# Quarter loads of the down projection on GpSimd's queue, its seven-product groups later, one transposed block turned later

## Chip, cores and metric

The kernel runs on one core of one Trainium2 chip. The metric is the device time of one execution in microseconds (us), lower is better; the time of a version is the median of its runs.

## What is computed

One layer of a decoder trunk, 256 tokens, 2048 channels, all float32:

```
h = rmsnorm(x) * w;  proj = h @ w_in                        # 2048 x 14368
two token mixers (gated delta rule, causal pooling) from proj, merged by gates -> mixed
x = x + mixed @ w_out                                       # 2048 x 2048
h = rmsnorm(x) * w
gate, up = split(h @ w_up)                                  # 2048 x 2*5632
gate = causal depthwise conv(gate, 3 taps) + bias
x = x + (gelu(gate) * up) @ w_down                          # 5632 x 2048
y = rmsnorm(x) * w_final
```

The change touches the last output block of `mixed @ w_out`, the start of `h @ w_up`, and the product with `w_down`.

## The kernel before

**Products.** TensorE multiplies in float32r. To keep float32 accuracy, each operand is split into a high part and a low part (value less high part). For one weight block of 256 rows x 512 columns (two slices of 128 rows), each of the two token tiles of 128 takes six matmuls of 512 columns: high x high, low x high and high x low for each slice (`products`, L1295, for the down projection; `high_first`, used at L1313, for up). So a plain block is 12 matmuls.

**Weights.** All blocks of the whole kernel stand in one list, `srcs`, in the order in which TensorE uses them. `weights()` (L167) hands out the next block and makes sure that blocks two further on are begun. `begin` (L240) does for each block: load it (SP issues the DMA, 512 KB, L179, into one of four `raw` buffers), copy the high part on ACT (`whi`, L253), subtract on VectorE (`wlo`, L261). There are three buffers each of `whi` and `wlo`, so a cast waits until TensorE is through with the block three before it. A block that is used at the very end is kept in a buffer of its own (`khi`, `klo`), cast among the others.

**Seven products.** In three of the eleven 512-row chunks of the down projection (`SEVEN`, chunks 8, 9 and 10), a 2 x 2 product of halves is done with seven products instead of eight: 11, 21, 22, T1, T3, T2, T4 (`PRODUCTS`), six matmuls each. This needs sums on both sides:
- of the weights: two loads of 1 MB each (`quad`, L209, in the big buffers x1 and x2) bring four quarters of 256 x 512; VectorE forms the four sums in place (L246), and each of the seven is split like a block;
- of the tokens: `half_sums` (L1237) forms four sums on VectorE (L1226 to L1229) and splits them (L1230, L1231).

A quarter's buffer can be loaded again when the last product from it has been split: x1 after T3, x2 after T4. The buffers x1 and x2 held features 4 to 7 and 8 to 11 of the up projection before.

**Order of the down projection.** It goes in two halves of 1024 columns. `stream` (L128) lays out each half: `gaps` gives how many plain blocks come before each of the three groups, each product of a group but the first is followed by one plain block, and what is left of the 32 plain blocks of the first half comes last. Before: gaps (4, 2, 2) in the first half, (3, 1, 1) in the second, where four kept blocks are put in too. The last up tile's gate and up parts (transposes at L341, then `gate_part` and `up_part`) are done behind the first and second plain block. In the code, `quarter` issues the two loads when it is asked for "11", on SP; `half_sums` of the next group is called at the "11" of the group before it.

**Banks.** Results are summed in PSUM: `psm` (two buffers of two banks) and `psg` (four banks). In the first half 11, T1, T3 and T2 have the psg banks, which are freed by a chain of sums on VectorE after T4 of the third group; the second half's plain blocks sum in psg.

**The output projection.** It makes four blocks of 512 columns. For each: a product, the residual added on VectorE into `xt` (L1194), the sum stored to HBM (`xtd`, ACT's queue), squares on ACT, eight transposes on TensorE (L1204) into psg, and the high and low part of the features `fhl` (L1209, L1210). Then come the up blocks, whose first ones read features 0 to 3. The buffer of `xt` then serves for quarters of the up projection, and after the last of these the residual is read back from `xtd` with four loads on ACT (L1412); the weights of the last norm follow (`nfin`, L1414).

**Who orders.** Buffers, waits and the order on each engine come from a scheduler, which follows a timeline of its own and can pull an instruction ahead of its place in the code; for TensorE's up stage the order is written out by hand.

Of the kernel before, what the change touches and what calls it, by code (L numbers as in the profile page):

```python
# [8 lines left out]
F32 = mybir.dt.float32  # L9
# [3 lines left out]
ALU = mybir.AluOpType  # L13

P = 128
# [20 lines left out]
def kernel(  # L36
# [91 lines left out]
    def stream(half, direct, gaps, keeps=()):  # L128
        todo = [(kp, c) for d in direct for kp in (2 * d, 2 * d + 1) for c in (2 * half, 2 * half + 1)]
        used = [0]  # L130

        def plain(n):
            for _ in range(n):
                kp, c = todo.pop(0)
                steps[half].append(("plain", kp, c))
                srcs.append(down[c][kp])
                used[0] += 1
                if used[0] in keeps:
                    i = keeps.index(used[0])
# [12 lines left out]
        plain(len(todo))  # L152

    ends = [(2 * d + j, c) for d in LAST for c in (2, 3) for j in range(2)]
    stream(0, DIRECT, (4, 2, 2))
    stream(1, DIRECT[:-2], (3, 1, 1), (9, 13, 17, 21))
    srcs += [down[c][kp] for kp, c in ends[:4]]
    made = []
# [21 lines left out]

    quarters = {}
    up_quarters = {}
    last_quad_split = [None]
    UP_BUFFER = {"11": 0, "T1": 1, "T2": 1, "T3": 0, "21": 2, "22": 3, "T4": 1}

    def quad_load(c, n):
# [8 lines left out]
    def up_sum(what):  # L195
        b11, b12, b21, b22 = (up_quarters[i] for i in range(4))
        for out_, plus_, minus_ in {"T1": [(b12, b12, b11)], "T2": [(b12, b22, b12)],
                                    "T3": [(b11, b12, b11), (b12, b21, b12)]}[what]:
            nc.vector.tensor_tensor(out_, plus_, minus_, op=ALU.subtract)  # L199

    def quarter(half, chunk, what):

        if half == "up":
            return up_quarters[UP_BUFFER[what]]
        if what == "11":
            for j in range(2):
                r = big.tile([P, 2, 1024], F32, tag=f"x{1 + j}", name=nm("quad"))
                rows = slice((2 * chunk + j) * 256, (2 * chunk + j + 1) * 256)
                last_load[0] = nc.sync.dma_start(r, w_down[0, rows, half * 1024 : (half + 1) * 1024]  # L209
                                                 .rearrange("(k p) f -> p k f", p=P)).ins  # L210
                for i in range(2):
                    quarters[j, i] = r[:, :, 512 * i : 512 * (i + 1)]
        b11, b12, b21, b22 = (quarters[j, i] for j in range(2) for i in range(2))
        sums = {"T1": (b11, b12, b11), "T3": (b12, b22, b12), "T2": (b22, b22, b11), "T4": (b21, b21, b22)}
        return sums[what] if what in sums else quarters[int(what[0]) - 1, int(what[1]) - 1]
# [24 lines left out]
    def begin(n):  # L240
        while len(made) < min(len(srcs), n):
            load(len(made) + 1)
            raw = loads[len(made)]
            if isinstance(raw, tuple):
                raw, plus, minus = raw
                nc.vector.tensor_tensor(raw, plus, minus, op=ALU.subtract)  # L246
            src = srcs[len(made)]
            following = {"T1": "T2", "T2": "T3"}.get(src[2]) if isinstance(src, tuple) and src[0] == "up" else None
            shape = list(raw.shape)
            keep = kept.get(len(made))  # L250
            hi = wpool.tile(shape, F32R, tag="whi", name=nm("whi")) if keep is None else \
                mtile(keep, shape, F32R, nm("khi"))
            nc.scalar.copy(hi, raw)  # L253
            if shape[1] == 8:
                lo = None
                nc.vector.tensor_tensor(hi[:, :, 32:64], raw[:, :, 0:32], hi[:, :, 0:32].bitcast(F32),
                                        op=ALU.subtract)
            else:
                lo = wpool.tile(shape, F32R, tag="wlo", name=nm("wlo")) if keep is None else \
                    mtile(4 + keep, shape, F32R, nm("klo"))  # L260
                last_split[0] = nc.vector.tensor_tensor(lo, raw, hi.bitcast(F32), op=ALU.subtract).ins  # L261
                splits.append(last_split[0])
            made.append((hi, lo))
            if following is not None:
                up_sum(following)
            if isinstance(src, tuple) and src[2] == "T4":
                last_quad_split[0] = last_split[0]


    side_work = [iter(())]  # L270
# [8 lines left out]
    def pm():  # L279
        return psm.tile([P, 2, 512], F32, tag="m", name=nm("psm"))  # L280
# [114 lines left out]
    def both(parts, k):  # L395
        return parts[k // 4][:, k % 4]
# [791 lines left out]
    for c in range(4):  # L1188
        if c < 2:
            ps = gemm_a(at(mhi), at(mlo), KD, range(6, 8), early[c])  # L1190
        else:
            ps = gemm_a(at(mhi), at(mlo), KD)
        xs = xt[:, :, c * 512 : (c + 1) * 512]
        nc.vector.tensor_tensor(xs, xs, ps, op=ALU.add)  # L1194
        nc.scalar.dma_start(xt_d[:, :, c * 512 : (c + 1) * 512], xs)
        for t in range(2):
            jk = cpool.tile([P, 512], F32, tag="sqj", name=nm("sqj"))
            nc.scalar.activation(jk, xs[:, t, :], AF.Square, accum_out=ssq4[:, t, c : c + 1])
        for k2 in range(2):
            pt = pg([P, 2, S])  # L1200
            for kk in range(2):
                k = 4 * c + 2 * k2 + kk
                for t in range(2):
                    nc.tensor.transpose(pt[:, kk, t * P : (t + 1) * P], xt[:, t, k * P : (k + 1) * P], ident)  # L1204
            for kk in range(2):
                k = 4 * c + 2 * k2 + kk
                nw = vec[:, V_FFN + k : V_FFN + k + 1]
                high, low = (both(fhl, k)[:, n, :] for n in range(2))
                nc.scalar.activation(high, pt[:, kk, :], AF.Copy, scale=nw)  # L1209
                nc.vector.scalar_tensor_tensor(low, pt[:, kk, :], nw, high.bitcast(F32),  # L1210
                                               op0=ALU.mult, op1=ALU.subtract)
# [169 lines left out]
    for i, step in enumerate(up_steps):  # L1381
        if step[0] == "part":
            up_product(*step[1:])
            if step[2] == "T4":
                def elementwise(c=step[1] - 1, gates=gates, ups=ups):
                    yield from gate_part(c, gates)
                    up_part(c, ups)
                    yield

                work[:] = [elementwise()]  # L1390
        elif step[0] == "gate":
            gates = turned_pair(pending[step[1], 0])
        elif step[0] == "up":
            ups = turned_pair(pending[step[1], 1])
        elif step[0] == "plain":
            up_plain(*step[1:])
            if step[1] == 0 and step[2:] == (0, TAIL):
                up_ups.append(up_sums())
            if step[1] == NUP - 1 and step[2:] == (0, KD // 2 - 1):
                half_sums(SEVEN[0])  # L1400
            if work:
                next(work[0], None)
        for n in range(4):
            if i + 8 - n < len(up_steps) and up_steps[i + 8 - n][0] == "loads":
                quad_load(up_steps[i + 8 - n][1], n)
        if i + 3 < len(up_steps) and up_steps[i + 3][0] == "loads":
            up_sum("T1")
    pe_order.close()

    xt = fp.tile([P, 2, D], F32, tag="xt", name="xt")  # L1410
    for c in range(4):
        nc.scalar.dma_start(xt[:, :, c * 512 : (c + 1) * 512], xt_d[:, :, c * 512 : (c + 1) * 512])  # L1412
# [32 lines left out]
    for hf in range(2):  # L1445
# [9 lines left out]
            bank_of |= zip(("11", "T1", "T2", "T3"), other)  # L1455
        began = set()
        for n, step in enumerate(steps[hf]):
            if hf == 0 and n == 1:
                for _ in gate_part(NUP - 1, turned(pending[NUP - 1, 0])):
                    pass  # L1460
# [13 lines left out]
            chunk, what = step[1:]  # L1474
            if what not in bank_of:
                bank_of[what] = pg()
            if hf == 0 and what == "11" and chunk != SEVEN[-1]:
                half_sums(SEVEN[SEVEN.index(chunk) + 1])
            which = OPERAND[what]
            if isinstance(which, tuple):  # L1480
# [117 lines left out]
```

## Time and profile before

| | us |
|---|---|
| median of 3 runs (lowest, highest) | 1553.15 (1551.57, 1554.37) |
| the profiled execution | 1552.89 |
| its span | 1551.2 |
| TensorE (PE) busy | 1538.3 |
| VectorE (DVE) busy | 1195.5 |
| ScalarE (ACT) busy | 827.5 |
| GpSimd (POOL) busy | 44.7 |
| output projection ends, up stage begins | at about 818 |
| down projection begins | at about 1306 |
| last products end | at about 1537 |

The granted TensorE clock is full but for the last stretch. HBM is read at 199 GB/s on average over the span. The profile comes from one execution. Times in it are counted from the start of its span. Rows of the timeline have start, duration, engine, line, operation, out<-in, shapes, count, and in brackets the engine's idle time ahead of it and what ended it. PEld is TensorE's weight load, SPq and ACTq are instructions of SP's and ACT's queue, that issue DMAs. Matmul ends are modelled, so pauses of TensorE are best read from the starts.

### The profile page before, as it was taken

What the parts mean: (1) busy time and instruction counts of PE and PEld (TensorE: products, weight loads), DVE (VectorE), ACT (ScalarE), POOL (GpSimd) and SP (SyncE); (2) the same over time, 40 slices, a digit from 0 to 9 for tenths busy, and PEclk for the clock granted to TensorE, in tenths of its full rate; (3) what the DMA queues carried; (4) which work ended last, traced back from release to release, by engine and by line L of the source; (5) the groups of instructions that cost most, each with busy time, mean ns of one, the idle gap of its engine ahead of it and who ended that gap; (6) DMA issues with size and microseconds to landing.
All of it is one profiled execution on the core that took longest, in us unless ns stands there. A gap on an engine that the chain in (4) does not pass through costs nothing.

```text
span 1551.2 us, 20085 instructions
## 1 busy us (share of the span) xinstructions
PE 1538.3 (99%) x7350; PEld 1267.7 (82%) x7350; DVE 1195.5 (77%) x1712; ACT 827.5 (53%) x1038; POOL 44.7 (3%) x54
## 2 busy tenths in 40 slices
PE   9999999999999999999999999999999999999998
PEld 8888888788878888888887888888888888788786
DVE  6788858996689858886665777777778776977875
ACT  6455446454545446454554666655666655554552
POOL 1010002000100000000000000000000000000000
PEclk9999999999999999999999999999999999999999
DMA  8776757676576756675667555455655557456562
GB/s 273 210 224 208 202 154 226 214 207 181 165 237 208 206 164 202 216 206 177 221 215 254 180 192 182 163 192 203 204 203 200 181 167 281 172 188 224 202 210 90
DMA packets 168017, 310.45 MB, mean 200 GB/s; under 512 B 19266, under 2 KB 23138, under 8 KB 167790
## 3 DMA queue, kind: packets, MB, share of 16 engines
q1 hardware_dynamic: 162720, 299.95, 60.2%
q10 hardware_dynamic: 5198, 9.23, 1.8%
q8 instruction: 57, 0.93, 0.2%
q14 instruction: 42, 0.34, 0.1%
HBM read 301.75 MB, written 7.38 MB: 199 GB/s over the span
## 4 chain that ended last, share of the span: by engine, by line
PE 93%; DMA 3%; DVE 2%; issue 1%; ACT 1%; POOL 0%; POOLq 0%; DVEq 0%; ACTq 0%
PE psg L1313 28%; PE psm L298 14%; PE psm L296 14%; PE psm L297 14%; PE psm L1298 7%; PE psg L1298 5%; PE psm L439 1%; PE psm L1370 1%; PE psg L341 1%; DVE wlo L261 1%; PE psm L1313 1%; DMA vrow<-ev 1%; DMA raw<-in_w_up_dram 1%; PE psg L829 1%; ACT whi L253 1%
## 5 line engine op out<-in xcount | busy, mean ns | idle before, releaser
L253 ACT CAST whi<-raw 128x1024 fp32r<-128x1024 f32 x460 | 483.5, 1052 | 486.7 <-PE psm L297 275.7
L261 DVE TENSOR_TENSOR wlo<-raw,whi 128x1024 fp32r<-128x1024 f32 x458 | 556.4, 1220 | 174.0 <-ACT whi L253 167.1
L298 PE MATMUL psm<-wlo,xhl 128*128 128x512 f32 x864 | 339.6, 393 | 0.9 <-DVE wlo L261 0.9
L296 PE MATMUL psm<-whi,xhl 128*128 128x512 f32 x864 | 338.6, 392 | 0.0
L297 PE MATMUL psm<-whi,xhl 128*128 128x512 f32 x864 | 337.9, 391 | 0.0
L1313 PE MATMUL psg<-whi,fhl 128*128 128x512 f32 x1208 | 302.1, 390 | 0.6 <-ACT whi L253 0.6
L1313 PEld LDWEIGHTS psg<-whi,fhl 128*128 128x128 f32 x1208 | 225.8, 188 | 47.7 <-ACT whi L253 1.4
L261 DVE TENSOR_TENSOR wlo<-quad,whi 128x1024 fp32r<-128x1024 f32 x112 | 137.1, 1224 | 73.0 <-ACT whi L253 71.8
L298 PEld LDWEIGHTS psm<-wlo,xhl 128*128 128x128 f32 x864 | 162.2, 188 | 35.3 <-DVE wlo L261 2.1
L297 PEld LDWEIGHTS psm<-whi,xhl 128*128 128x128 f32 x864 | 162.2, 188 | 33.5
L296 PEld LDWEIGHTS psm<-whi,xhl 128*128 128x128 f32 x864 | 162.3, 188 | 33.3 <-issue 0.2
L253 ACT CAST whi<-quad 128x1024 fp32r<-128x1024 f32 x112 | 118.1, 1055 | 101.7 <-PE psg L1313 55.9
L1313 PE MATMUL psg<-wlo,fhl 128*128 128x512 f32 x604 | 164.0, 389 | 0.0
L1313 PEld LDWEIGHTS psg<-wlo,fhl 128*128 128x128 f32 x604 | 113.4, 188 | 23.6
L1298 PE MATMUL psm<-wlo,hhi 128*128 128x512 f32 (+1 forms) x150 | 57.9, 388 | 0.4 <-DVE wlo L261 0.4
L1298 PE MATMUL psm<-whi,hhi 128*128 128x512 f32 (+1 forms) x150 | 58.2, 388 | 0.0
L1298 PE MATMUL psm<-whi,hlo 128*128 128x512 f32 (+1 forms) x150 | 58.0, 386 | 0.0
L199 DVE TENSOR_TENSOR quad<-quad 128x1024 f32<-128x1024 f32 x40 | 49.0, 1225 | 6.6 <-DMA quad<-in_w_up_dram 5.6
L1298 PE MATMUL psg<-whi,hhi 128*128 128x512 f32 (+1 forms) x130 | 50.3, 387 | 0.8 <-ACT whi L253 0.8
L296 PE MATMUL psm<-whi,mhi 128*128 128x512 f32 x128 | 50.9, 397 | 0.0
L1298 PE MATMUL psg<-whi,hlo 128*128 128x512 f32 (+1 forms) x130 | 50.2, 386 | 0.0
L298 PE MATMUL psm<-wlo,mhi 128*128 128x512 f32 x128 | 50.0, 390 | 0.0
(336 smaller groups left out, 1699.5 us busy)
## 6 DMA issues: line engine op xcount, KB each, us to landing
raw<-in_w_in_dram SPq DMA_DIRECT2D x224, 512.0 KB, 4.3
raw<-in_w_up_dram SPq DMA_DIRECT2D x136, 512.0 KB, 4.6
raw<-in_w_down_dram SPq DMA_DIRECT2D x64, 512.0 KB, 4.7
quad<-in_w_up_dram SPq DMA_DIRECT2D x40, 512.0 KB, 6.5
raw<-in_w_out_dram SPq DMA_DIRECT2D x32, 512.0 KB, 4.1
quad<-in_w_down_dram SPq DMA_DIRECT2D x12, 1024.0 KB, 6.5
mv<-vrow SPq DMA_DIRECT2D x12, 512.0 KB, 4.7
taps<-in_conv_qkv_w_dram SPq DMA_DIRECT2D x16, 256.0 KB, 6.9
```

The costliest lines, as they stand in the source:

```text
L199: nc.vector.tensor_tensor(out_, plus_, minus_, op=ALU.subtract)
L253: nc.scalar.copy(hi, raw)
L261: last_split[0] = nc.vector.tensor_tensor(lo, raw, hi.bitcast(F32), op=ALU.subtract).ins
L296: mm(ps[:, t, :], lh(k, t), hi[:, kk, :], start=(k == 0), stop=False)
L297: mm(ps[:, t, :], ll(k, t), hi[:, kk, :], start=False, stop=False)
L298: mm(ps[:, t, :], lh(k, t), lo[:, kk, :], start=False, stop=(k == nk - 1))
L341: nc.tensor.transpose(pt[:, ff, t * P : (t + 1) * P], src[:, t, f * P : (f + 1) * P], ident)
L439: mm(ps_k0[:, t, :], part(k, t), w[:, kk, :], start=(k == 0 and w is hi and part is xh), stop=(k == KD - 1 and w is lo))
L829: mm(pg0, kq[:, h, 0, 0:P], kq[:, h, :, :], start=True, stop=True)
L1298: mm(ps[:, cs], lhs(kk), part_[:, kk, cs], start=(first and kk == 0 and n == 0), stop=(last and kk == 1 and n == 2), skip_group_check=shared)
L1313: mm(ps, lhs(kk), w[n][:, kk], start=(first and n == 0 and kk == 0 and lhs is high), stop=False, skip_group_check=True)
L1370: nc.tensor.transpose(out_[f // 2][:, f % 2, t * P : (t + 1) * P], e[:, t, f * P : (f + 1) * P], ident)
```

## The change

Four things are edited:
1. In the fourth output block the transposes and the split of the features are put into a function, `turned_rows`, which is called after the second up block (step ("plain", 0, 0, 1)); its result goes to one psm buffer instead of two psg banks.
2. The gaps of the first half become (6, 3, 3).
3. The two quarter loads of a group are issued by GpSimd. The first group's are called for at the first step of the down projection, each later group's as soon as T4 of the group before has been split.
4. `half_sums` of the next group is called at T4 instead of 11; the four loads that read the residual back are called for two by two at 11 of the second and of the third group.

```diff
-    stream(0, DIRECT, (4, 2, 2))
+    stream(0, DIRECT, (6, 3, 3))
...
+    groups = [(half, chunk) for half in range(2) for chunk in SEVEN]
+
+    def next_group():
+
+        if groups:
+            half, chunk = groups.pop(0)
             for j in range(2):
                 r = big.tile([P, 2, 1024], F32, tag=f"x{1 + j}", name=nm("quad"))
                 rows = slice((2 * chunk + j) * 256, (2 * chunk + j + 1) * 256)
-                last_load[0] = nc.sync.dma_start(r, w_down[0, rows, half * 1024 : (half + 1) * 1024]
-                                                 .rearrange("(k p) f -> p k f", p=P)).ins
+                nc.gpsimd.dma_start(r, w_down[0, rows, half * 1024 : (half + 1) * 1024]
+                                    .rearrange("(k p) f -> p k f", p=P))
...
-            if isinstance(src, tuple) and src[2] == "T4":
-                last_quad_split[0] = last_split[0]
+            if isinstance(src, tuple) and src[0] != "up" and src[2] == "T4":
+                next_group()
...
+        def turned_rows(c=c, xt=xt):
+            shared = pm() if c == 3 else None
+            for k2 in range(2):
+                pt = pg([P, 2, S]) if shared is None else shared[:, k2].rearrange("p (k s) -> p k s", k=2)
...
+        if c < 3:
+            turned_rows()
...
             up_plain(*step[1:])
+            if step[1:] == (0, 0, 1):
+                turned_rows()
...
-    for c in range(4):
-        nc.scalar.dma_start(xt[:, :, c * 512 : (c + 1) * 512], xt_d[:, :, c * 512 : (c + 1) * 512])
...
+            if hf == n == 0:
+                next_group()
...
-            if hf == 0 and what == "11" and chunk != SEVEN[-1]:
+            if hf == 0 and what == "11" and chunk != SEVEN[0]:
+                for c in range(2):
+                    cs = slice((2 * SEVEN.index(chunk) - 2 + c) * 512, (2 * SEVEN.index(chunk) - 1 + c) * 512)
+                    nc.scalar.dma_start(xt[:, :, cs], xt_d[:, :, cs])
+            if hf == 0 and what == "T4" and chunk != SEVEN[-1]:
                 half_sums(SEVEN[SEVEN.index(chunk) + 1])
```

More of the change, by code (lines that the diff above doesn't have):

```diff
@@ L182 @@
     up_quarters = {}
-    last_quad_split = [None]
     UP_BUFFER = {"11": 0, "T1": 1, "T2": 1, "T3": 0, "21": 2, "22": 3, "T4": 1}
@@ L199, in up_sum @@
             nc.vector.tensor_tensor(out_, plus_, minus_, op=ALU.subtract)
+    groups = [(half, chunk) for half in range(2) for chunk in SEVEN]
+    def next_group():
+        if groups:
+            half, chunk = groups.pop(0)
+            for j in range(2):
+                r = big.tile([P, 2, 1024], F32, tag=f"x{1 + j}", name=nm("quad"))
+                rows = slice((2 * chunk + j) * 256, (2 * chunk + j + 1) * 256)
+                nc.gpsimd.dma_start(r, w_down[0, rows, half * 1024 : (half + 1) * 1024]
+                                    .rearrange("(k p) f -> p k f", p=P))
+                for i in range(2):
+                    quarters[j, i] = r[:, :, 512 * i : 512 * (i + 1)]
     def quarter(half, chunk, what):
@@ L204, in quarter @@
             return up_quarters[UP_BUFFER[what]]
[L205 to L209, printed above, removed]
-                                                 .rearrange("(k p) f -> p k f", p=P)).ins
-                for i in range(2):
-                    quarters[j, i] = r[:, :, 512 * i : 512 * (i + 1)]
         b11, b12, b21, b22 = (quarters[j, i] for j in range(2) for i in range(2))
@@ L1198 @@
             nc.scalar.activation(jk, xs[:, t, :], AF.Square, accum_out=ssq4[:, t, c : c + 1])
[L1199 to L1211, printed above, removed]
+        def turned_rows(c=c, xt=xt):
+            shared = pm() if c == 3 else None
+            for k2 in range(2):
+                pt = pg([P, 2, S]) if shared is None else shared[:, k2].rearrange("p (k s) -> p k s", k=2)
+                for kk in range(2):
+                    k = 4 * c + 2 * k2 + kk
+                    for t in range(2):
+                        nc.tensor.transpose(pt[:, kk, t * P : (t + 1) * P], xt[:, t, k * P : (k + 1) * P], ident)
+                for kk in range(2):
+                    k = 4 * c + 2 * k2 + kk
+                    nw = vec[:, V_FFN + k : V_FFN + k + 1]
+                    high, low = (both(fhl, k)[:, n, :] for n in range(2))
+                    nc.scalar.activation(high, pt[:, kk, :], AF.Copy, scale=nw)
+                    nc.vector.scalar_tensor_tensor(low, pt[:, kk, :], nw, high.bitcast(F32),
+                                                   op0=ALU.mult, op1=ALU.subtract)
+        if c < 3:
+            turned_rows()
     ssq2 = cpool.tile([P, 2], F32, name="ssq2")
```

## The prediction

> **What bounds the kernel now.** I read the page from its first part down: busy time, then the chain that ended last, then that chain in order of time.
>
> ```profile
> PE 1538.3 (99%) x7350; PEld 1267.7 (82%) x7350; DVE 1195.5 (77%) x1712; ACT 827.5 (53%) x1038; POOL 44.7 (3%) x54
> PE 93%; DMA 3%; DVE 2%; issue 1%; ACT 1%; POOL 0%; POOLq 0%; DVEq 0%; ACTq 0%
> 918.78 25.86 PE psg L1313 x114
> 1309.40 0.87 PE psg L341 x8
> ```
>
> TensorE is the bound: the chain lies on it for 93%. In the up stage 114 products in a row take 25.86 us, 0.2268 us each, and eight transposes 0.87 us, 0.109 each. The change takes no product away, so only pauses can be won, stretches in which two starts lie further apart than 0.227. Going through the starts of TensorE from 805 us on, I find five places. The change claims four and leaves one as it is.
>
> **The last residual block.** The timeline of TensorE, ACT and VectorE at the end of the output projection:
>
> ```profile
> 818.23 0.39 PE L298 MATMUL psm<-wlo,mhi 128*128 128x512 f32 x1
> 819.93 1.09 PE L1204 MATMUL psg<-ident,xt 128*128 128x128 f32 x8 [1.32 <-DVE xt L1194]
> 818.43 1.04 ACT L253 CAST whi<-raw 128x1024 fp32r<-128x1024 f32 x1 [1.67 <-PE psm L297]
> 818.66 1.22 DVE L1194 TENSOR_TENSOR xt<-xt,psm 128x1024 f32<-128x1024 f32 x1 [0.64 <-PE psm L298]
> 819.79 1.22 DVE L261 TENSOR_TENSOR wlo<-raw,whi 128x1024 fp32r<-128x1024 f32 x1
> ```
>
> The last product starts at 818.23, the transposes at 819.93 although TensorE was free at 818.46: they wait for the residual addition, which ends at 819.88. That is 1.47 us. In the new order two up blocks (24 products, 5.44 us) stand before the transposes, so these are asked for at about 823.9, 4 us after the addition. Is anything else late? The cast at 818.43 and the subtraction at 819.79 are those of the third up block, since three high tiles exist and the first two were made before; so the first two blocks can start at 818.46. They read features 0 to 3, the late block is features 12 to 15, first read by the tenth block, about 24 us on. The transposes now go to a psm buffer whose last reader was the addition of the third output block. On the queues: the buffer that holds the residual also takes the first four quarter loads of the up stage, so they follow the transposes, about 4 us later, and two raw loads now pass them on SP. Their first use is a whole up tile away. **Gain 1.47, taken whole**; if that cover failed, it would show as a pause of the same size in the first up tile.
>
> **Token sums and groups later.** Two stretches of equal length (columns: length, then busy time and instructions of PE, PEld, DVE, ACT, POOL, clock, DMA share, GB/s), and VectorE and TensorE inside the first:
>
> ```profile
> 1306.50:1337.18 30.68, 30.03 (x135) 23.38 (x134) 28.45 (x36) 18.45 (x22) 0.00 (x0) 1.00 0.41 143
> 1337.18:1367.86 30.68, 30.68 (x137) 25.42 (x137) 24.82 (x23) 16.64 (x17) 0.00 (x0) 1.00 0.65 227
> 1322.18 1.22 DVE L261 TENSOR_TENSOR wlo<-raw,whi 128x1024 fp32r<-128x1024 f32 x1
> 1323.32 1.28 DVE L1283 TENSOR_TENSOR y<-psg,y 128x512 f32<-128x512 f32 x2
> 1324.52 0.41 DVE L1229 TENSOR_TENSOR sums<-whole,sums 128x256 f32<-128x256 f32 x1
> 1324.85 1.22 DVE L261 TENSOR_TENSOR wlo<-quad,whi 128x1024 fp32r<-128x1024 f32 x1
> 1322.40 0.63 PE L1298 MATMUL psm<-whi,sx 128*128 128x512 f32 x2
> 1323.45 0.50 PE L1298 MATMUL psm<-wlo,hhi 128*128 128x512 f32 x1 [0.43 <-DVE wlo L261]
> 1323.79 0.40 PE L1298 MATMUL psm<-whi,hhi 128*128 128x512 f32 x1
> ```
>
> The first stretch holds 16 transposes (as much as 7.7 products) and 119 products, the second 137 products: 10.3 fewer, 2.3 us, of which some 0.2 goes where products start again behind the two sets of transposes, and stays. So 2.1 us of pauses, with VectorE busy 93% of it: the end of the last up tile, the token sums and the first group's weight sums fall together.
>
> What the diff says and what is built differ here. In the built order the token sums of the second and third group stand as early on VectorE as before; moving the call to T4 does nothing, since the scheduler pulls them up. What acts is two more plain blocks ahead of the first group: 5.44 us more for TensorE. But VectorE now has more before the subtraction on which TensorE first waited (end 1323.40, asked for at 1322.85, 0.60 late with its start): four more 128x1024 instructions (two plain blocks, the last hidden block's low part, the first sums' low part) at 1.14 from start to start, the two up products at 1.20 and a sum at 0.33, together 6.09. So it is 0.60 + 6.09 - 5.44 = 1.25 late, and 0.11 goes at the restart (1323.45 to 1323.79 is 0.34, not 0.23). Those instructions lie behind that point in the old order, so the later pauses go. **Gain 2.1 - 1.36 = 0.7**, between 0 and 2.1.
>
> At the other end fewer plain blocks are left: three instead of seven between T4 of the third group and the second half, whose banks the third group's sums must free.
>
> ```profile
> 1402.62 1.23 DVE L261 TENSOR_TENSOR wlo<-quad,whi 128x1024 fp32r<-128x1024 f32 x1 [1.27 <-ACT whi L253]
> 1408.62 0.68 DVE L1500 TENSOR_TENSOR u<-u,psg 128x512 f32<-128x512 f32 x1
> ```
>
> From T4's subtraction to the last freed bank is 6.7 us; T4 (1.36) and three blocks (8.16) are 9.5. Covered by 2.8 us: cost nothing; without the cover the missing time.
>
> **Quarter loads on GpSimd.** No DMA is issued by POOL in the trace, so its price is bounded. First what the loads cost now: the second half's second and third groups.
>
> ```profile
> 1454.20 0.37 SPq L209 DMA_DIRECT2D quad<-in_w_down_dram  x1
> 1456.46 2.18 SPq L179 DMA_DIRECT2D raw<-in_w_down_dram  x2
> 1461.00 1.05 ACT L253 CAST whi<-quad 128x1024 fp32r<-128x1024 f32 x1 [2.65 <-DMA quad<-in_w_down_dram]
> 1464.36 1.05 ACT L253 CAST khi<-raw 128x1024 fp32r<-128x1024 f32 x1 [2.31 <-DMA raw<-in_w_down_dram]
> 1465.26 0.39 PE L1298 MATMUL psg<-wlo,hhi 128*128 128x512 f32 x1
> 1466.40 0.50 PE L1298 MATMUL psg<-whi,hhi 128*128 128x512 f32 x1 [0.76 <-ACT whi L253]
> 1478.01 3.77 SPq L179 DMA_DIRECT2D raw<-in_w_down_dram  x2
> 1484.86 1.05 ACT L253 CAST khi<-raw 128x1024 fp32r<-128x1024 f32 x1 [2.25 <-DMA raw<-in_w_down_dram]
> 1487.73 0.39 PE L1298 MATMUL psg<-whi,hlo 128*128 128x512 f32 x1
> 1488.36 0.50 PE L1298 MATMUL psg<-wlo,hhi 128*128 128x512 f32 x1 [0.24 <-DVE wlo L261]
> 1490.28 1.06 ACT L253 CAST whi<-quad 128x1024 fp32r<-128x1024 f32 x1 [1.52 <-PE psg L1298]
> DMA to landing us min/median/max: 5.5/6.5/7.1
> ```
>
> Both pauses (from 1465.26 on 1.14 less 0.23, with 0.11 for the restart 1.0; from 1487.73 on in the same way 0.5) have one cause: ACT casts in order, and a raw block behind a 1 MB quarter load lands late, 1484.86 for a load of 1478.01. The issue itself won't be earlier: 1454.20 is where T4's subtraction of the group before frees the buffer, and the POOL order waits for the same subtraction. SP is not relieved either, as the next raw load (1456.46) waits for a raw buffer of its own. What changes is the queue: raw blocks need not stand behind the quarters.
>
> How late may a quarter come? At 1461.00 its cast ends 2.31 us before the next one can start, so up to 2.3 us more cost nothing there. In the third group the cast at 1490.28 waits for TensorE, not for its load. If the quarter shares the 16 DMA engines with the raws behind it, it ends no later than these do now, 3.4 us on (1464.36 against 1461.00); with POOL equal to SP the delay is 0. I take 1.5, hidden by the 2.31. The third group's raw then doesn't stand behind a whole megabyte: **gain 0.5**, between 0 and 0.5. In the second group the last raw waits for all bytes in flight, so only a better filled DMA helps:
>
> ```profile
> 1302.50:1311.50 9.00, 9.00 (x46) 7.53 (x45) 4.89 (x5) 5.08 (x8) 0.00 (x0) 1.00 0.98 371
> 1455.50:1464.30 8.80, 8.80 (x40) 7.31 (x39) 6.83 (x6) 3.16 (x3) 0.00 (x0) 1.00 0.70 242
> ```
>
> 242 GB/s against 371 in a stretch with queues full. At 371 the 2.1 MB would take 5.7 us instead of 8.8 and the pause would be gone; with no better rate nothing is won. **I take half, 0.5**, between 0 and 1.0. A page speaks against it: the Trainium skill, DMA: Bandwidth & Descriptors, "Issuing engines are not separate DMA queues", says that DMAs run on the same 16 engines whoever issues them and that spreading them saves only issue time; by it this gain is nothing and the sum 2.7. No run here shows a POOL queue yet.
>
> The first half's groups have four blocks (10.9 us) between T4 and their first use, over 7.1, the longest landing; the first group's loads, on SP at 1295 and 1301, are asked for after 1319. POOL has nothing behind the twelve loads but the two small powers of the tail.
>
> **The residual's reload.** The diff moves four 512 KB loads of xt to the second and third group. In the built order they stand on ACT exactly where they stood, with the same waits.
>
> ```profile
> 1268.87 1.91 ACTq L1412 DMA_DIRECT2D xt<-xtd  x3
> 1271.51 11.44 DMA raw<-in_w_up_dram
> 1282.66 1.07 PE L1313 MATMUL psg<-wlo,fhl 128*128 128x512 f32 x4
> 1283.04 1.05 ACT L253 CAST whi<-raw 128x1024 fp32r<-128x1024 f32 x1 [5.71 <-DMA raw<-in_w_up_dram]
> 1284.14 2.11 PE L1313 MATMUL psg<-whi,fhl 128*128 128x512 f32 x8 [0.41 <-ACT whi L253]
> 1287.33 0.96 PE L1313 MATMUL psg<-whi,fhl 128*128 128x512 f32 x3 [0.18 <-ACT whi L253]
> ```
>
> They fill the DMA when a raw block is due, which takes 11.44 us. Four products from 1282.66 end at 1283.57, and the next starts 0.57 later; twelve from 1284.14 with a restart would end at 1286.97, and the next starts 0.36 later; with restarts 1.1 us. This stays: 0.
>
> **Sum.** 1.47 + 0.7 + 0.5 + 0.5 = 3.2 us. The profiled execution took 1552.89 us (span 1551.2 and 1.7 around it), 0.26 under the median 1553.15. So 1549.7 on its scale, **1550.0 us** as a median. A measurement of this kernel tells about 0.2% (3.1 us) from no change, which puts the bound at 1550.05: my forecast lies on it.
>
> **Rivals.** Only the transposes count: VectorE is 93% busy in the first group, and if its order slips by 0.7 us nothing is won there, nor by the other queue. 1553.15 - 1.47 = 1551.7. For it: the smallness of the cover on VectorE. Against: 5.44 us of new slack.
>
> All claimed pauses go: 1.47 + 2.1 + 1.0 + 0.5 = 5.1, 1548.1. Against: the 1.25 counted above.
>
> Late quarters, which ends slower: descriptors made by GpSimd bring each quarter so late that both tight groups of the second half wait. Above 2.3 us of delay each pays one for one. With 4.7 (the longest landing above, 11.44, less the 6.7 of the quarter of 1454.20) it is 2 x 2.4 = 4.8 less 2.2 for the first two parts: 1555.8. It outweighs them from a delay of 3.4, a landing about 10 us after the issue.
>
> GpSimd held up by VectorE: VectorE is busy 6.83 of 8.80 us in the stretch from 1455.50; if descriptors waited for one or two to end, 1.2 to 2.4 us come on top of 1.5, 0.4 to 1.6 over the slack in two groups, and the last two gains go: 1553.15 - 2.2 + 2.0 = 1553.0. The Trainium skill, SBUF — State Buffer, "Who interferes with whom", has such a lock for two-port modes of VectorE, but says that tensor_tensor takes only the read side, which descriptor writing doesn't need; the trace shows no case.
>
> The change does what it says with the reload (1.1 more, 1548.9): only if the built order is not what runs.
>
> **How the numbers follow.** Forecast 0.45 (1549.0 to 1551.2), only the transposes 0.2, all pauses 0.14, late quarters 0.12, GpSimd held up 0.07, reload 0.02. The forecast's chance is split on the bound, a little over half to the faster side; with the other two fast cases and a part of what lies between, faster 0.46, same 0.38, slower 0.16 (late quarters and the tail of the held up case). The range reaches from all pauses gone, 1547.7 with the spread of the runs, to 1554.0, leaving most of the late quarters outside.
>
> **What would show it.** Right: up products right behind the last L298, transposes with no idle ahead; one pause of about 1.3 in the first group; no raw wait of ACT near the third group. Wrong: casts of quad blocks waiting over 2.3 us longer on a POOL queue; pauses at the second half's start; the 1.1 us of the reload gone. The forecast falls if quarters land over 9 us after issue.

## The result

The changed kernel is slower: 1555.59 us (median of 20 runs, 1552.25 to 1557.04) beside 1552.64 for the kernel before (20 runs), ratio 1.0015, 95% interval 1.0008 to 1.0022, so 1.2 to 3.4 us. I had forecast 1550.0 with a range to 1554.0; neither holds. The profiled execution took 1555.6 us with a span of 1553.9, 2.7 more than before.

The page after, busy times and the chain that ended last:

```profile
PE 1537.2 (99%) x7350; PEld 1268.1 (82%) x7350; DVE 1195.2 (77%) x1712; ACT 828.8 (53%) x1038; POOL 53.6 (3%) x66
PE 95%; DMA 2%; DVE 1%; issue 1%; ACT 1%; POOL 0%; POOLq 0%; ACTq 0%; DVEq 0%
```

TensorE has the same 7350 instructions and is still the bound; the busy times tell nothing of the 2.7 us. What tells is the start of each TensorE instruction less the time that the instructions ahead of it need (0.2268 us for 512 columns). The growth of this over a stretch is what TensorE lost there; worked out from the starts in both traces, in us:

| stretch | before | after | change | forecast |
|---|---|---|---|---|
| up to the output projection's end | | | +0.26 | 0 |
| late transposes, first up blocks | 1.99 | 3.15 | +1.16 | -1.47 |
| end of the up stage (reload) | 2.20 | 2.00 | -0.20 | 0 |
| first group, first half | 2.13 | 1.40 | -0.73 | -0.7 |
| start of the second half | 0 | 0.31 | +0.31 | 0 |
| ahead of the second group, second half | 1.14 | 2.64 | +1.50 | -0.5 |
| ahead of the third group, second half | 0.55 | 0.46 | -0.09 | -0.5 |

The rows sum to 2.2; 0.1 more is lost between the second and the third row, and 0.4 behind the last product. The first group is as forecast; two rows make the loss. The first is the late transposes (timeline after):

```profile
818.72 1.98 PE L1324 MATMUL psg<-whi,fhl 128*128 128x512 f32 x8
824.17 0.60 PE L1212 MATMUL psm<-ident,xt 128*128 128x128 f32 x4
824.80 0.47 ACT L1217 ACTIVATE fhl<-psm,vec 128x256 fp32r<-128x256 f32 x1 [0.30 <-PE psm L1212]
825.68 0.48 DVE L1218 SCALAR_TENSOR_TENSOR fhl<-psm,vec,fhl 128x256 fp32r<-128x256 f32 x1
826.19 0.47 ACT L1217 ACTIVATE fhl<-psm,vec 128x256 fp32r<-128x256 f32 x1 [0.91 <-DVE fhl L1218]
826.70 0.48 DVE L1218 SCALAR_TENSOR_TENSOR fhl<-psm,vec,fhl 128x256 fp32r<-128x256 f32 x1 [0.54 <-ACT fhl L1217]
827.24 0.66 PE L1212 MATMUL psm<-ident,xt 128*128 128x128 f32 x4 [2.47 <-DVE fhl L1218]
```

The up products do start at once behind the last L303 (818.49), and the first four transposes wait for nothing: the 1.47 us are gone. But before, eight transposes stood in a row; now there are four, and four more 2.47 us of idle time later. They write into the second half of the psm tile that ScalarE and VectorE are still reading the first half of, and wait for the last of these four evacuations, which ends at 827.18. From start to start it is 2.74 us where 0.06 is due: a pause of 2.69 for one of 1.47.

The second row, the pause ahead of the second group of the second half, is a raw block that lands late (chain of waits after):

```profile
1459.17 7.56 DMA raw<-in_w_down_dram
```

It is the raw block of a kept product (tile khi), 7.56 us from issue to landing; the casts stand in order on ScalarE, and TensorE pauses 2.42 us until 1468.79. The experiments ask whether GpSimd's queue makes it late.

### The profile page after: what moved, and what is told of

Same layout as the page of the kernel before. It is cut to its first block, busy times and chain, and to the rows that moved or that the text cites. A ratio compares the mean times of both kernels' runs of the same rounds, so it can differ in the third digit from the quotient of the medians.

```text
span 1553.9 us, 20103 instructions
## 1 busy us (share of the span) xinstructions
PE 1537.2 (99%) x7350; PEld 1268.1 (82%) x7350; DVE 1195.2 (77%) x1712; ACT 828.8 (53%) x1038; POOL 53.6 (3%) x66
## 4 chain that ended last, share of the span: by engine, by line
PE 95%; DMA 2%; DVE 1%; issue 1%; ACT 1%; POOL 0%; POOLq 0%; ACTq 0%; DVEq 0%
PE psg L1324 29%; PE psm L303 14%; PE psm L301 14%; PE psm L302 14%; PE psm L1309 7%; PE psg L1309 6%; PE psm L444 1%; PE psm L1381 1%; PE psg L346 1%; PE psm L1324 1%; DMA vrow<-ev 1%; PE psg L834 1%; DVE wlo L266 1%; DMA mv<-vrow 1%; DMA raw<-in_w_down_dram 0%
## 5 line engine op out<-in xcount | busy, mean ns | idle before, releaser
L303 PE MATMUL psm<-wlo,xhl 128*128 128x512 f32 x864 | 339.7, 393 | 1.4 <-DVE wlo L266 1.4
L303 PEld LDWEIGHTS psm<-wlo,xhl 128*128 128x128 f32 x864 | 162.3, 188 | 35.7 <-DVE wlo L266 2.6
L303 PE MATMUL psm<-wlo,mhi 128*128 128x512 f32 x128 | 50.0, 390 | 0.0
```

The costliest lines, as they stand in the source:

```text
L303: mm(ps[:, t, :], lh(k, t), lo[:, kk, :], start=False, stop=(k == nk - 1))
```

## The experiments

Each run was timed in five rounds beside the kernel before on the same chip; the ratio is to that. Theory at first: two losses, the split of the transposes and the quarters' queue.

**1. Eight transposes in a row** (first rival: ScalarE and VectorE are short of time there).

```diff
         def turned_rows(c=c, xt=xt):
...
+            pts = []
             for k2 in range(2):
...
+                pts.append(pt)
+            for k2, pt in enumerate(pts):
                 for kk in range(2):
```

> The changed kernel, with one edit: in turned_rows all eight transposes are issued ahead of the four evacuations, so the second four no longer write into a psm tile whose first half is still being read. Theory (the pause of 2.69 us at 824.49 is only the wait of the second four transposes for the readers of the same tile): the pause goes, eight transposes stand in one row, 1555.6 - 2.7 = 1552.9 us. Rival (ScalarE and VectorE are short of time there, and the pause only shows it): a pause of 1 us or more comes back in the first up tile, where products wait for casts or low parts, and the time stays above 1554.5.

Measured 1551.10 us, ratio 0.9990 (0.9981 to 0.9999): faster than before, and 4.5 us under the changed kernel (3.9 by the two ratios), more than the pause. Its timeline:

```profile
823.70 1.04 PE L1213 MATMUL psm<-ident,xt 128*128 128x128 f32 x8
824.49 2.07 PE L1327 MATMUL psg<-whi,fhl 128*128 128x512 f32 x8
824.77 0.47 ACT L1220 ACTIVATE fhl<-psm,vec 128x256 fp32r<-128x256 f32 x1 [0.74 <-PE psm L1213]
```

No pause, and products follow 0.79 us after the first transpose; the same evacuations are spread among casts behind them and nobody waits. The rival falls. The wait was one on the tile: the same two halves, the same banks, and only the order of issue differs. That the medians differ by 4.5 where the pause is 2.69 stayed open.

**2. Quarter loads on SyncE again, and 3. both edits.**

```diff
         if half == "up":
             return up_quarters[UP_BUFFER[what]]
+        if what == "11":
+            next_group()
...
-                nc.gpsimd.dma_start(r, w_down[0, rows, half * 1024 : (half + 1) * 1024]
+                nc.sync.dma_start(r, w_down[0, rows, half * 1024 : (half + 1) * 1024]
```

(the two other calls of next_group are taken out)

> The changed kernel, with one part undone: the quarter loads of the down projection go out on SyncE's queue again, at the first product of their group. Theory (the quarters start late on GpSimd's queue, and the raw blocks behind them come late for it): the pauses of 2.42 us at 1466.15 and 0.17 at 1438.18 fall back to about 0.9 and 0, 1555.6 - 1.8 = 1553.8 us. Rival (the new distance of the groups, not the queue, makes that pause): it stays above 2, and the time at 1555.6.

> The edits of the two kernels before together: eight transposes in a row, quarter loads on SyncE's queue. If the two losses are independent, 1555.6 - 2.7 - 1.8 = 1551.1 us, which is before less the residual block's pause (1.47) and most of 0.74 in the first group: 1550.4 by that count. If each frees only time that the other loses, 1552.5 or more.

Measured 1555.57 (ratio 1.0017, 1.0008 to 1.0026) and 1550.92 (0.9990, 0.9982 to 0.9999): each as its twin with the quarters on GpSimd. The theory of the late quarters falls; that run 3 meets its 1551.1 is luck, since the 1.8 us for the queue are not there and the medians of runs 2 and 3 differ by 4.65, not 2.7. The late raw block in the chains of run 2 (quarters on SyncE), run 1 and run 15 (both on GpSimd, the same kernel):

```profile
1458.84 7.30 DMA raw<-in_w_down_dram
```

```profile
1455.66 5.80 DMA raw<-in_w_down_dram
```

```profile
1457.66 7.46 DMA raw<-in_w_down_dram
```

One kernel on one queue gives 5.80 and 7.46 us. In the six profiles of this document with the quarters on SyncE and the second half unchanged up to its second group, the pause there is 0.92 to 2.17 us (mean 1.44); in nine with GpSimd 0.57 to 2.42 (mean 1.52). So these profiles show no difference by the queue. They do show another one: of the six profiles in which the transposes are split with TensorE idle in between, five have 2.0 us or more at this pause; of the nine others one has (run 15, 2.29). How a pause at 824 could do that 640 us later is not shown, and with so few profiles it may be chance; that the 0.92 before and the 2.42 after are two draws of the same lot is not shown either.

**4. The reload really moved.** In the changed kernel it stands where it stood (four loads from 1270.4 to 1272.4).

```diff
-            nc.scalar.copy(hi, raw)
+            last_high[0] = nc.scalar.copy(hi, raw).ins
...
+                with tc.issue_after(last_high[0]):
                     for c in range(2):
```

(and the same for nfin, in the second group)

> The changed kernel, with the residual's reload and the final norm's weights really issued in the second and third group of seven (each held behind the latest cast on ScalarE); in the changed kernel they stand where they stood before. Theory (they keep the raw block of the last up tile late): the two pauses at 1284.84 and 1288.09, 0.73 us together, go, and nothing new comes: 1554.9 us. Rival (the reload takes the DMA from the quarters of the second and third group): products there wait, 1556.5 or more.

Measured 1554.79, ratio 1.0009 (1.0001 to 1.0018). In the trace of run 4 the products of 1282.65 to 1292 stand without a gap; these two waits of the changed kernel are gone:

```profile
1285.46 2.12 PE L1324 MATMUL psg<-whi,fhl 128*128 128x512 f32 x8 [0.23 <-ACT whi L258]
1288.65 2.12 PE L1324 MATMUL psg<-whi,fhl 128*128 128x512 f32 x8 [0.17 <-ACT whi L258]
```

As the theory had it in the trace; the 0.8 us in the medians is inside their uncertainty. Runs 8 and 10, with the same edit, have no such wait either; of the 14 profiles without it, 13 have at least one. In this profile the pause ahead of the second group is 2.37 us, and products behind it stand 0.427 apart for some 3 us: a first sign of the clock.

**5. The distances alone** (the kernel before with one line).

```diff
-    stream(0, DIRECT, (4, 2, 2))
+    stream(0, DIRECT, (6, 3, 3))
```

> The kernel before, with one part of the change: six, three and three plain blocks ahead of the groups of the first half instead of four, two and two. Theory (this part gives its 0.7 us in the first group and 0.3 back where the second half starts, and has nothing to do with the third group of the second half): one pause of 1.27 us in the first group, 1552.8 - 0.4 = 1552.4 us. Rival (the new distance makes the long pause in the third group of the second half): a pause of 2.2 or more there, 1553.7 us.

Measured 1551.95, ratio 0.9993 (0.9984 to 1.0001). One pause of 1.27 in the first group, 0.31 lost at the second half's start, 0.99 ahead of the second group, which the text calls the third: the theory, and in this profile the distances do not delay that raw block.

**6 to 10. A block more in front of the late raw block, other distances.** Runs 6 and 7 change (3, 1, 1) of the second half to (3, 1, 2), run 6 on run 1, run 7 on the changed kernel. I had the pause ahead of the wrong group there; run 9 is run 1 with (3, 2, 1). Run 8 is run 6 and run 10 is run 9 with (7, 2, 3) in the first half and the late reload.

> The changed kernel with all eight transposes ahead of their evacuations, and with two plain blocks instead of one between the second and the third group of the second half. Theory (raw blocks there are issued at the same distance every time, and land 5.8 to 7.8 us later, as the DMA serves them; one block more, 2.72 us, covers the worst of it): no pause in the third group, 1551.0 - 0.7 to 1551.0 - 1.9, say 1549.7 us. Rival (the raw blocks' issue moves along with the products, so that they are as late as before): a pause of 0.7 or more stays, 1551 us.

> The changed kernel as it is, with the one block more ahead of the third group of the second half. With that pause out of the way, the distance to the run with eight transposes in a row is the price of the split transposes alone. Theory A (2.7 us, the pause that the trace shows; what the two kernels differed by beyond it was the DMA's luck in the third group): 1549.7 + 2.7 = 1552.4 us. Theory B (the split costs 4.5 us, with something later that hangs on it): 1554.2 us.

> The kernel with eight transposes in a row and one block more ahead of the third group of the second half, and with two further edits: seven, two and three plain blocks ahead of the groups of the first half, and the reload of the residual and the final norm's weights issued in the second and third group. Theory (each plain block ahead of the first group gives TensorE 2.72 us and VectorE 1.14 of work, so the 1.27 us pause of the first group goes; the 0.4 to 1.1 us of the reload too): 1549.7 - 1.3 - 0.7 = 1547.7 us. Rival (the second group, one block earlier, and the reload beside its quarters, make a new pause of 1 us or more): 1549 us or more.

> The changed kernel with all eight transposes ahead of their evacuations, and two plain blocks instead of one between the first and the second group of the second half. The pause of 0.66 to 2.42 us at about 1465 stands there, ahead of the second group; the texts of the earlier runs called it the third, and the block put in ahead of the third group could not cover it. Theory (the raw block there lands 5.8 to 7.8 us after its issue, and one block more covers most of that): pause under 0.3 there, 1551.0 - 1.2 = 1549.8 us. Rival (the issue of the raw blocks moves along with the products): 0.7 or more stays, 1551 us.

> As the run before, with seven, two and three plain blocks ahead of the groups of the first half, and with the reload and the final norm's weights issued in the second and third group. In the earlier run with these two edits, the first group had no pause and the second one of 0.62 us, and the two of the last up tile were gone. If they add up with the block ahead of the second group: 1549.8 - 0.65 - 0.5 = 1548.6 us. If the pauses come back elsewhere: 1551 us.

Measured 1552.00, 1555.41, 1551.51, 1552.66 and 1553.41 us (ratios 0.9993, 1.0017, 0.9992, 0.9997, 0.9998, each within 0.0010 either way). None beats run 1, and the gains forecast for runs 6, 8, 9 and 10 did not come. The block of runs 6 and 7 brings pauses of 0.53 and 0.71 ahead of the third group; in run 9 the wait changes place and shrinks to 0.38 and 0.60:

```profile
1466.62 1.05 ACT L258 CAST khi<-raw 128x1024 fp32r<-128x1024 f32 x1 [3.65 <-DMA raw<-in_w_down_dram]
1469.62 0.50 PE L1312 MATMUL psg<-whi,hhi 128*128 128x512 f32 x1 [0.21 <-ACT whi L258]
1471.25 0.50 PE L1312 MATMUL psg<-wlo,hhi 128*128 128x512 f32 x1 [0.43 <-DVE wlo L266]
```

The number of run 9's rival holds (0.7 or more stays), its mechanism only in part: the raw block is issued 8.8 us ahead of the last product before the pause (1460.17 for 1469.01), 7.0 in run 1 (1455.66 for 1462.64).

Run 8 did not clear the first group, although the text of run 10 says so. Its product 11 starts at 1324.21, and both pauses, 1.07 and 0.62 us, lie inside that group:

```profile
1328.45 0.50 PE L1313 MATMUL psm<-whi,hhi 128*128 128x512 f32 x1 [0.91 <-ACT whi L259]
1337.84 0.50 PE L1313 MATMUL psm<-whi,hhi 128*128 128x512 f32 x1 [0.46 <-ACT whi L259]
```

Together they are 1.69 for the 1.27 of six plain blocks: with the seventh block the group loses more, not less, here to casts on ScalarE. Run 10 has the same two pauses and one of 2.02 that ends at 1498.39.

Runs 6 and 7 differ by 3.4 us; that speaks for theory B, and the trace of run 7 shows it: its loss at the late transposes is 4.48, not 3.15, with products 0.427 apart behind the pause.

**11 and 12. The late transposes alone**, distances and quarters as before: in a row as in run 1, and split as in the change.

> Of the change only the late transposes, and these with all eight ahead of their evacuations; distances of the groups and quarter loads as before. If the 1.47 us pause of the last residual block goes and nothing else moves: 1552.8 - 1.5 = 1551.3 us. If ScalarE and VectorE are late with what they have to do beside the first up blocks: a new pause, 1552 us or more.

> Of the change only the late transposes, as the change has them: four, their evacuations, four more into the same tile. Theory A (the price is the pause of 2.7 us alone): 1551.3 + 2.7 = 1554.0 us. Theory B (TensorE's clock drops to a half after the pause in a part of the executions, which costs 1.3 to 1.6 us more in each of these, at this pause and at the one ahead of the second group of the second half where it is as long): the profile may show a granted clock of 0.5 behind one of them, and the median is 1554.5 to 1555.5 us.

Measured 1551.51 (ratio 0.9988, 0.9979 to 0.9997) and 1557.00 (1.0025, 1.0015 to 1.0035). Moving them gives what I had forecast, 1.47, within the interval (0.5 to 3.3 us), and in the trace 0.43 us are lost there for 1.99; splitting them costs 5.5 us more. Run 12 in its timeline:

```profile
823.30 0.60 PE L1212 MATMUL psm<-ident,xt 128*128 128x128 f32 x4
826.37 0.66 PE L1212 MATMUL psm<-ident,xt 128*128 128x128 f32 x4 [2.47 <-DVE fhl L1218]
826.78 3.39 PE L1324 MATMUL psg<-whi,fhl 128*128 128x512 f32 x8
```

Eight products take 3.39 us for 2.07 in run 1. The stretches of 2 us of run 12 (the clock is the third column from the end):

```profile
824.00:826.00 2.00, 0.00 (x0) 0.00 (x0) 1.46 (x3) 0.88 (x2) 0.00 (x0) 1.00 0.81 266
826.00:828.00 2.00, 1.63 (x8) 1.39 (x9) 0.74 (x2) 0.47 (x1) 0.00 (x0) 0.81 0.90 256
828.00:830.00 2.00, 2.00 (x7) 1.51 (x6) 0.54 (x2) 0.47 (x1) 0.00 (x0) 0.50 0.76 200
830.00:832.00 2.00, 2.00 (x9) 1.64 (x8) 0.54 (x1) 1.05 (x1) 0.00 (x0) 0.84 1.04 404
1470.00:1472.00 2.00, 2.00 (x6) 1.58 (x5) 2.00 (x2) 0.29 (x1) 0.00 (x0) 0.50 0.84 257
```

and of the changed kernel's profile:

```profile
826.00:828.00 2.00, 0.76 (x6) 0.72 (x7) 0.64 (x2) 0.54 (x2) 0.00 (x0) 1.00 0.82 251
828.00:830.00 2.00, 2.00 (x10) 1.66 (x9) 0.97 (x2) 1.10 (x3) 0.00 (x0) 1.00 0.80 223
```

The same idle time of 2.47 us; in one execution the clock falls to 0.50 behind it, in the other it stays at 1.00. The loss over the late transposes is 4.75 for 3.15. Run 12 has a second fall behind the pause ahead of the second group.

**13 to 15. The pause filled**, beside the changed kernel and run 1 repeated on one chip (runs 14 and 15).

```diff
             for k2 in range(2):
+                if shared is not None and k2:
+                    fill = pm()[:, 0]
+                    for n in range(24):
+                        mm(fill[:, :S], both(fhl, 0)[:, 0, :P], both(fhl, 0)[:, 0, :], start=True, stop=True)
```

> The changed kernel, with 24 products of 256 columns (2.72 us by 0.2268 for 512) between the first four and the second four late transposes; they write to a psm tile that nobody reads. The wait stays as long, but TensorE is busy in it. Theory (TensorE's clock falls to a half behind the pause in some executions): without the pause no such fall there, so only the 2.7 us are paid: 1 to 1.8 us faster than the changed kernel on the same chip, 2.7 to 3.2 slower than with eight transposes in a row. Rival (the split costs 4.5 us whether TensorE is idle or busy in it): as the changed kernel.

> The changed kernel itself, beside the other two on one chip. 1555.6 us as before. Its profile is another draw: if the clock falls in a part of the executions, the granted clock behind the transposes may be 0.5 this time; without that the pause is 2.7 us.

> The kernel with eight transposes ahead of their evacuations, beside the other two on one chip: 4.5 us faster than the changed kernel if that distance is real (1551.1), 2.7 if the rest was the chips' luck (1552.9). Its pause ahead of the second group of the second half, 0.66 us in the first profile, is another draw: under 1.4 if the long pauses there hang on the split, up to 2.4 if they are luck.

Measured 1553.19 (ratio 0.9998, 0.9989 to 1.0007), 1554.61 (1.0008, 0.9999 to 1.0017) and 1551.22 (0.9989, 0.9980 to 0.9998). Run 13:

```profile
823.36 0.60 PE L1216 MATMUL psm<-ident,xt 128*128 128x128 f32 x4
823.72 3.11 PE L1211 MATMUL psm<-fhl 128*128 128x256 f32 x24
826.66 0.60 PE L1216 MATMUL psm<-ident,xt 128*128 128x128 f32 x4
827.02 2.09 PE L1328 MATMUL psg<-whi,fhl 128*128 128x512 f32 x8
```

The second four transposes come no earlier, but 2.7 us of needless products make the kernel 1.4 us faster than run 14, in the span forecast for the clock; that distance is about as large as its uncertainty. The pause ahead of the second group is short too in its profile, 0.88 for 2.22 in run 14, so the clock is not the only candidate for the 1.4. The single times stand further apart: the 11 of run 13 lie between 1552.20 and 1553.86; the 20 of the changed kernel lie in two heaps, 8 from 1552.25 to 1554.47 and 12 from 1555.43 to 1557.04. Over run 15, run 13 is 2.0 us slower, under the forecast 2.7 to 3.2. Run 14 shows the pause of 2.69 without a fall, run 15 a pause of 2.29 ahead of the second group with one: such a long pause can come without the split. That it comes no more often with it is not shown (run 2 above).

## Why the prediction was wrong, point by point

- **The last residual block** is the step that failed. "The transposes now go to a psm buffer whose last reader was the addition of the third output block" is true of the first four only. Both sets now share one tile, so the last readers ahead of the second four are the evacuations of the first four; the built order has a wait on VectorE at the fifth transpose, and I read the order of the transposes without it. In place of a gain of 1.47 the trace shows a loss of 1.16 (3.15 for 1.99). The gain itself is real: without the split it came (run 11). The price of the split, 2.7 us in every trace, is shown by run 1.
- **What the pause brings with it** I did not weigh at all: TensorE's clock. It falls to 0.50 in 2 of the 6 profiles with the split, and each fall costs 1.3 to 1.6 us. That it makes the upper heap of the changed kernel's times is not shown, and that kernel's own two profiles speak against it as the only cause: their executions took 1555.57 and 1556.55 us, in the upper heap, with no fall. Both have a pause of over 2.2 us ahead of the second group.
- **Token sums and groups later**: right in mechanism and size. I had 1.25 late and 0.11 at the restart; the trace has one pause, behind a subtraction that starts at 1329.57:

```profile
1329.57 1.21 DVE L266 TENSOR_TENSOR wlo<-raw,whi 128x1024 fp32r<-128x1024 f32 x1
1330.84 0.50 PE L1309 MATMUL psm<-wlo,hhi 128*128 128x512 f32 x1 [1.11 <-DVE wlo L266]
```

  The gain is 0.73 for a forecast 0.7. The end of the half, costed at nothing with a cover of 2.8 us, costs 0.31, also in run 5: not through the banks, but through a product at 1438.58 that waits for a cast on ScalarE (1437.47 to 1438.53) and the restart behind it.
- **Quarter loads on GpSimd**: the gains of 0.5 and 0.5 are not there. Runs 2 and 3 differ from their twins by 0.02 and 0.18 us, with each ratio uncertain by about 1.4 us. By the Trainium skill, DMA: Bandwidth & Descriptors, "Issuing engines are not separate DMA queues", they were nothing too; the two mean pauses of 1.44 and 1.52 agree. The fear behind my slower rivals was as wrong: in the second half the quarters landed 5.3 to 7.3 us after issue on GpSimd's queue, 6.5 to 7.6 on SyncE's in run 2; one of the first half of the changed kernel took 9.5, over the 9 that the prediction named as its end, and TensorE did not pause for it. The time of the rival of late quarters, 1555.8, is close to the measured one by coincidence; its mechanism did not occur.
- **The reload stays**: right; run 4 shows that moving it takes its pauses away.
- The sum thus had one term of the wrong sign (1.47 forecast, -1.16), two that the runs do not show, and a price behind the pause that was missing.

What stays open: the medians of split and unsplit kernels differ by 3.4 to 5.5 us, of which the trace explains 2.7 and a part of 1.6 for each fall of the clock; each median is uncertain by about 1 us, and how often the clock falls was not counted beyond the profiles. Whether the split also lengthens the pause ahead of the second group is open, and so is the cause of the two heaps.

## What to carry to other kernels

Where two sets of writes go to one tile instead of two, read the order with its waits: issue all the writes first, or give each set its own tile. An idle TensorE can cost more than its idle time, here from 1.84 us in one window of the clock on (next section), so a bound from the start-to-start pause is a lower bound. Before a term is claimed from one landing time, see whether other profiles of the same order give the same; here one pause ranged from 0.57 to 2.42 us.

## What the runs showed of the hardware

- TensorE's clock fell to 0.50 behind idle times of 2.47 us (run 12; 2 of 6 such pauses) and of 1.84 us ahead of 1468.45 (run 12 again), and products stood 0.427 us apart instead of 0.227 for about 3 us. Of 13 pauses of 2.0 us or more in these profiles it fell behind 5. What decides is where the pause lies: in each trace the clock changes only at times that are whole multiples of 3.413 us apart (in run 12 at 827.22, 830.64, 1468.93 and 1472.34), and each of the five falls lasts one such window. Here are windows that hold a pause, each but the last with the window behind it, from run 12 (two pauses), run 7, run 4 and the changed kernel (length and busy time of TensorE first, clock third from the end):

```profile
823.81:827.22 3.41, 0.94 (x7) 0.81 (x7) 1.96 (x3) 1.10 (x3) 0.03 (x1) 1.00 0.85 240
827.22:830.63 3.41, 3.41 (x10) 2.62 (x9) 0.97 (x2) 1.21 (x3) 0.00 (x0) 0.50 0.87 278
1465.52:1468.92 3.40, 1.56 (x7) 0.99 (x6) 2.30 (x3) 2.52 (x3) 0.00 (x0) 1.00 0.01 3
1468.93:1472.34 3.41, 3.41 (x10) 2.64 (x9) 3.41 (x4) 1.36 (x2) 0.00 (x0) 0.50 0.61 183
822.34:825.75 3.41, 1.46 (x9) 1.01 (x7) 2.23 (x6) 2.00 (x3) 0.70 (x1) 1.00 0.85 280
825.76:829.16 3.40, 2.89 (x9) 2.50 (x10) 1.14 (x3) 0.95 (x2) 0.00 (x0) 0.50 0.68 194
822.10:825.51 3.41, 1.72 (x10) 1.24 (x8) 2.48 (x5) 1.79 (x3) 0.69 (x1) 1.00 0.90 283
825.52:828.92 3.40, 2.62 (x14) 2.24 (x15) 1.36 (x3) 1.24 (x4) 0.00 (x0) 1.00 0.72 222
825.86:829.27 3.41, 2.03 (x11) 1.77 (x12) 1.26 (x3) 1.26 (x3) 0.00 (x0) 1.00 0.84 271
```

  Idle times of 2.47, 1.84 and 1.95 us in one window bring the fall, 1.69 and 1.38 don't, though the pause at the split is 2.47 us long each time. In all 17 profiles, between 8 and 1535 us, the clock falls behind every window with 1.84 us or more of idle time (five) and behind none with 1.69 or less; what lies between, about half a window, was not met. If the place of the pause in the window is random, an estimate from these figures is that a pause of 2.47 us brings a fall in about two executions of three; the six profiles have two. The Trainium skill, TensorE: Matmul & The Clock Gate, "What's actually happening", names at least one idle window of about 3.4 us, on a window that runs freely. The free window fits the 3.41 us found here and that the same pause does it in one execution and not in the next; that it takes a whole window of idleness does not fit 1.84 and 2.47 us, and the measurement decides.
- A quarter on GpSimd's queue held back the raw blocks issued behind it on SyncE's. In the changed kernel, raw blocks were issued at 1457.35 and 1459.17, and between 1458 and 1460 the DMA moved the quarter of 1455.36 alone (packets, MB, share of the engines):

```profile
q0 software_dynamic: 176, 0.71, 94.1%
```

  SyncE's first packets of these blocks come between 1460 and 1461, 4 of them. Run 1 has the same between 1454.5 and 1456.5 (quarter of 1451.86, a raw block issued at 1453.85):

```profile
q0 software_dynamic: 196, 0.78, 96.4%
```

  At these two places two queues acted like one queue in order, which fits that the second gave nothing.
